# The state-space pipeline of a hybrid decoder step: output one tick later and into the state's tile, two places for the input product, paired matrices

## Chip, cores, metric

The kernel runs on one core of a Trainium2 chip. The metric is device time in microseconds (us), the median of several runs. One further execution was recorded by the hardware profiler; all rows shown come from it.

## What is computed

One inference step of a decoder layer over 2048 + 16 prompt positions and 8 running sequences of 8 tokens, 1024 channels, in fp32. An input projection gives six streams. One of them goes through a state-space branch (64 groups of 16 channels, 64 complex states each), one through a pooling branch (causal means over 2, 4, 8 or 16 positions, one window for each quarter of the channels); gates, two branch projections and an output projection follow.

```
...
    bu_re = jnp.einsum('blgc,gpc->lbgp', uf, bbar_re)
...
    _, _, s_re, s_im = lax.associative_scan(
        _complex_scan_combine, (a_seq_re, a_seq_im, bu_re, bu_im), axis=0)
...
    y = (jnp.einsum('lbgp,gcp->blgc', s_re, c_re.astype(f32))
         - jnp.einsum('lbgp,gcp->blgc', s_im, c_im.astype(f32)))
    y = y.reshape(bsz, seq_len, D_SSM) + d.astype(f32) * uf.reshape(bsz, seq_len, D_SSM)
...
        win = (cs[:, POOL_BUF + 1:POOL_BUF + 1 + seq_len, lo:hi]
               - cs[:, POOL_BUF + 1 - w:POOL_BUF + 1 - w + seq_len, lo:hi])
...
    merged = g_s * (a @ w_branch_ssm) + g_p * (b @ w_branch_pool)
    return h + merged @ w_out, new_re, new_im, new_buf
```

## The kernel before

**Units.** Positions are folded into chunks of T = 8 and cut into four column groups (`g0` to `g3`, some 512 to 544 columns each). The program is a list of some 340 units written out by hand; nearly all are one 128-row block of one projection for one column group: 8 blocks of the inner dimension, three matmuls each in a split of the weights into a high and a low part (`wh`, `wl`; L128, L130, L132), each matmul in two column halves. TensorE goes through the units in order. What follows a unit (activations, gates, splits) is written on ScalarE, VectorE and GpSimd at the start of the next one; some more work is hung at fractions of a unit. Each engine works strictly in the order in which its instructions were written, and SyncE issues all DMAs in one queue.

**Ticks.** The state-space branch runs beside the units as a software pipeline over 32 pairs of groups, in two rounds (the first for the columns of `g0`, `g1`, the second for `g2`, `g3` and the running sequences). A tick is one step of that pipeline and works on several pairs at once, each at another stage; 37 ticks a round are spread over the units by `spread`. In a unit with one tick, its EARLY part is written after a quarter of the unit's matmuls and its LATE part after the last. What a pair q goes through (number: ticks after its first):

- 0: `st_phase` (GpSimd), LATE `st_wrap` (VectorE), `st_load` (DMAs of the input `su` and the matrix `smb`)
- 1: `st_sin` (ScalarE), LATE `st_x`: the input product, four matmul records into PSUM tile `sx`
- 2: `st_turn_a` copies `sx` with its halves swapped (ScalarE L519, L520; in the second round also L522, the running sequences' part `xs`), `st_turn_v` multiplies `sx` by the cosines (VectorE L528), `st_turn_g` the copy by the sines (GpSimd); LATE `st_scan` (VectorE)
- 3: `st_swap` (ScalarE L546, L547, and the DMA of the matrices `smc`), LATE `st_rot` (VectorE)
- 4: `st_state` (GpSimd) writes the states `sS`, LATE `st_y`: `sy` = matrix times input (L577) plus matrix times state (L578), eight matmul records
- 5: `st_out` copies `sy` to `sY` (ScalarE L582), and a DMA takes that to `ys` in DRAM

In a tick ScalarE has, in this order: L582 for one pair, L546, L547 for a younger one, L519, L520 (L522) for a still younger one, then the sines. VectorE has L528 there. TensorE meets the tick at its LATE part: `st_y` first, then `st_x`. `sx` and `sy` are one PSUM tile each, `sY` and `sS` one SBUF buffer each, `su` four, `smb`, `smc`, `sX` and `sXw` two. Units with two ticks have both in halves of the unit.

**Matrices.** Each group's three 128x128 matrices are made early on, written to `mat_d` in DRAM in 512-byte rows, and read back pair by pair.

**Pooling.** `up_post` builds the window sums by doubling steps on VectorE (L820, L821, L822, L824).

Of the kernel before, what the change touches and what calls it, by code (L numbers as in the profile page):

```python
# [88 lines left out]
def hybrid_step(ctx, tc, a):  # L89
# [74 lines left out]
    mat_d = dram.tile([GRP, P, 3, P], F32, name="mat_d")  # L164
# [181 lines left out]
    def batches(bg):  # L346
# [51 lines left out]
        def s4(b):  # L398
# [9 lines left out]
                          ct[:, i, :, 0:7].rearrange("p c t -> p t c"), start=True, stop=True)  # L408
            d["ps"], d["pk"] = ps, pk

        def s5(b):
# [4 lines left out]
            SY.dma_start(mat_d[gs, :, 0].rearrange("g p m -> p g m"), btT)  # L416
            SY.dma_start(mat_d[gs, :, 2].rearrange("g p m -> p g m"), d["ct"].rearrange("p g c t -> p g (c t)"))
            o = 4 * (b % 2)
            A.activation(d["ks"][:, o:o + 4], d["pk"][:GCH], AF.Copy)

# [16 lines left out]
        def s10(b):  # L437
            o = 4 * (b % 2)
            mt = st.pop(b)["mt"]
            mp = bg.tile([P, 4, P], F32, tag="mp", name="mp")  # L440
            A.activation(mp.rearrange("p g (c t) -> p g c t", t=T),
                         mt[:, o:o + 4].rearrange("p g (t c) -> p g c t", c=GCH), AF.Copy)
            SY.dma_start(mat_d[4 * b:4 * b + 4, :, 1].rearrange("g p m -> p g m"), mp)

        S7 = [(7 + i, lambda b, i=i: s7(b, i)) for i in range(1, NPART)]
        load(0)
# [21 lines left out]
    def stile(tag, bufs, w=NA * NBB):  # L468
        return sw["p"].tile([P, 2, w], F32, tag=tag, bufs=bufs, name=tag)

    def two(q):
        return slice(2 * q, 2 * q + 2)
# [3 lines left out]
        return rows.rearrange("(q c) t k -> (c t) q k", q=2)  # L476

    def st_load(g, q):
        x = stile("su", 4, g.kn + NS)
# [27 lines left out]
    def st_x(g, q):  # L507

        d = pr[q]
        d["px"] = sw["sx"][:, :, :g.kn]  # L510
        for j in range(2):
            PE.matmul(d["px"][:, j], d["mb"][:, j], d["u"][:, j], start=True, stop=True)  # L512

    def st_turn_a(g, q):

        d = pr[q]
        ps, kp = d["px"], g.kp
        xw = stile("sXw", 2, kp)
        A.activation(xw[0:64], ps[64:128, :, :kp], AF.Copy)  # L519
        A.activation(xw[64:128], ps[0:64, :, :kp], AF.Copy)  # L520
        if g.last:
            A.activation(sw["xs"][:, two(q)], ps[:, :, kp:], AF.Copy)  # L522
        d["xw"] = xw

    def st_turn_v(g, q):
# [17 lines left out]
    def st_swap(g, q):  # L543
        d = pr[q]
        z, zw = d["x"], stile("sXw", 2, g.kp)
        A.activation(zw[0:64], z[64:128], AF.Copy)  # L546
        A.activation(zw[64:128], z[0:64], AF.Copy)  # L547
        d["xw"] = zw
        d["m"] = stile("smc", 2, 2 * P)
        SY.dma_start(d["m"].rearrange("p q (j m) -> p q j m", j=2),  # L550
                     mat_d[two(q), :, 1:3].rearrange("q p j m -> p q j m"))

    def st_rot(g, q):

# [5 lines left out]
    def st_state(g, q):  # L560

        d = pr[q]
        c, w, kp = d["c"], d["s"], g.kp
        s = stile("sS", 1, g.kn)
        now = state[:, two(q)].unsqueeze(2)
        if g.last:
            G.tensor_copy(s[:, :, kp:], d["s0"])
        G.tensor_copy(s[:, :, 0:1], now)
        G.tensor_tensor(s[:, :, 1:kp], c[:, :, 1:kp], w[:, :, 1:kp], ALU.subtract)  # L569
        G.tensor_tensor(now, c[:, :, kp:kp + 1], w[:, :, kp:kp + 1], ALU.subtract)  # L570
        d["S"] = s

    def st_y(g, q):
        d = pr[q]
        d["py"] = sw["sy"][:, :, :g.kn]
        for j in range(2):
            PE.matmul(d["py"][:, j], d["m"][:, j, :P], d["u"][:, j], start=True, stop=False)  # L577
            PE.matmul(d["py"][:, j], d["m"][:, j, P:], d["S"][:, j], start=False, stop=True)  # L578

    def st_out(g, q):  # L580
        y = stile("sY", 1, g.kn)
        A.activation(y, pr.pop(q)["py"], AF.Copy)  # L582
        SY.dma_start(chans(g, ys_d, q), y)

    EARLY = ((5, st_out), (3, st_swap), (2, st_turn_a), (1, st_sin), (4, st_state),
             (0, st_phase), (2, st_turn_v), (2, st_turn_g))
    LATE = ((3, st_rot), (0, st_wrap), (2, st_scan), (4, st_y), (1, st_x), (0, st_load))
    NTICK = NPAIR + 5  # L590
# [5 lines left out]

    def final_states():
        SY.dma_start(a["fin"], state)
        for j in range(2):
            s0 = tmp.tile([P, GRP, NS], F32, tag="po", bufs=2, name="s0")  # L600
            SY.dma_start(s0, a["s0"][:, j])
            G.tensor_tensor(s0, s0, a8[:, j].unsqueeze(2).to_broadcast([P, GRP, NS]), ALU.mult)
            G.tensor_tensor(sw["xs"], sw["xs"], s0, ALU.add)
        SY.dma_start(a["fins"], sw["xs"])

    mid = []

# [7 lines left out]
    class Group:  # L615
# [177 lines left out]
        def up_post(self, fb, ps):  # L793
            wi = fb // 2
            kn, kp, last = self.kn, self.kp, self.last
            ke = 2 + kp + (3 * NS if last else 0)
            E = self.t(tmp, "E", 2, shape=[P, T, ke])
            tn = T // self.nh
            if last:
                es = E[:, :, 2 + kp:].rearrange("p t (s k) -> p t s k", k=3)  # L800
                G.tensor_copy(es[:, :, :, 0:2], self.hs.pop(fb))
            for h in range(self.nh):
                src = ps[:, h, :self.N].rearrange("p (t k) -> p t k", k=kn)
                A.activation(E[:, h * tn:(h + 1) * tn, 2:2 + kp], src[:, :, :kp], AF.Copy)
                if last:
                    A.activation(es[:, h * tn:(h + 1) * tn, :, 2:3], src[:, :, kp:].unsqueeze(3), AF.Copy)
            G.tensor_copy(E[:, :, 0:2], hist[:, fb])  # L807
            if last:
                new = self.t(tmp, "np", 2, shape=[P, T, 2 + NS])
                G.tensor_copy(new[:, :, 0:2], E[:, :, kp:kp + 2])  # L810
                G.tensor_copy(new[:, :, 2:].unsqueeze(3), es[:, :, :, 2:3])
                SY.dma_start(a["np"][:, fb], new)
            else:
                G.tensor_copy(hist[:, fb], E[:, :, kp:kp + 2])
            cur = E
            for step in range(wi + 1):
# [597 lines left out]
```

## Time and profile before

| | |
|---|---|
| median of 3 runs | 2157.99 us (2157.77 to 2158.32) |
| profiled execution, its own time | 2159.06 us |
| its span, first to last instruction | 2157.3 us |
| TensorE busy | 2086.0 us, 97% |
| VectorE, GpSimd, ScalarE busy | 1395.2, 923.7, 686.8 us |

The profiled execution lies 1.1 us above the median, and 1.8 us of it lie outside the span. A wait in the profile is idle time of an engine just before an instruction, and is put down to what came last before that instruction could start.

### The profile page before, as it was taken

The numbers are of one execution on the slowest core, as the hardware profiler recorded it, in microseconds if no ns is written. First come the engines' busy times: TensorE is split into PE (matmuls) and PEld (weight loads), VectorE is DVE, ScalarE is ACT, GpSimd is POOL, SyncE is SP. The second block draws the span as 40 slices with busy tenths as digits, with TensorE's granted clock in tenths as the row PEclk, the third lists the DMA queues.
The fourth block names the chain that finished last, engine by engine and source line by source line (L and its number), as shares of the span: only waits on it lengthen the run. The fifth ranks groups of instructions, "written<-read, shape, count | busy, mean of one in ns | idle before, by whom it ended". The sixth has DMA issues, their size and how long they took to land.

```text
span 2157.3 us, 37693 instructions
## 1 busy us (share of the span) xinstructions
PE 2086.0 (97%) x14968; PEld 1970.9 (91%) x14968; DVE 1395.2 (65%) x1916; ACT 686.8 (32%) x1243; POOL 923.7 (43%) x1054
## 2 busy tenths in 40 slices
PE   7999999889899999999899999999999999999998
PEld 7988899888799999999899999999999987888887
DVE  7989968878656686644856676633633767456444
ACT  3213357645434332144544432121210221112101
POOL 3387747565444452233544452233421333244222
PEclk9999999999999999999999999999999999999999
DMA  6646556486944453244444543234333443343223
GB/s 199 145 117 165 164 169 200 144 202 155 183 127 124 151 144 120 89 121 137 120 125 144 157 139 125 82 119 118 104 100 109 144 128 120 101 133 117 91 97 105
DMA packets 261279, 287.77 MB, mean 133 GB/s; under 512 B 106096, under 2 KB 203760, under 8 KB 261104
## 3 DMA queue, kind: packets, MB, share of 16 engines
q1 hardware_dynamic: 261104, 285.37, 45.7%
q8 instruction: 118, 1.93, 0.4%
q14 instruction: 57, 0.47, 0.1%
HBM read 242.32 MB, written 40.62 MB: 131 GB/s over the span
## 4 chain that ended last, share of the span: by engine, by line
PE 71%; DVE 6%; DMA 4%; ACT 3%; issue 2%; POOL 2%; SPq 0%; DVEq 0%; ACTq 0%; POOLq 0%
PE acc L128 23%; PE acc L132 23%; PE acc L130 23%; DMA ys<-sY 1%; DVE wl L206 1%; DVE sX L537 1%; PE sy L578 1%; PE sx L512 1%; PE sy L577 1%; DVE sX L540 1%; DMA raw<-in_wb 1%; DVE al L114 1%; DVE sph L558 1%; DMA mat_d<-mp 1%; DVE sph L499 0%
## 5 line engine op out<-in xcount | busy, mean ns | idle before, releaser
L128 PE MATMUL acc<-ah,wh 128*128 128x268 f32 (+4 forms) x4504 | 1058.9, 305 | 8.9 <-ACT ah L705 6.6
L132 PE MATMUL acc<-ah,wl 128*128 128x268 f32 (+4 forms) x4504 | 1049.0, 302 | 3.7 <-DVE wl L206 3.7
L130 PE MATMUL acc<-al,wh 128*128 128x268 f32 (+4 forms) x4504 | 1047.9, 302 | 0.0
L103 POOL TENSOR_SCALAR wh<-raw 128x1024 fp32r<-128x1024 f32 (+1 forms) x336 | 392.5, 1168 | 969.9 <-PE acc L130 869.7
L128 PEld LDWEIGHTS acc<-ah,wh 128*128 128x128 f32 x4504 | 729.3, 190 | 44.2 <-issue 7.8
L132 PEld LDWEIGHTS acc<-ah,wl 128*128 128x128 f32 x4504 | 727.8, 189 | 32.0 <-DVE wl L206 4.7
L130 PEld LDWEIGHTS acc<-al,wh 128*128 128x128 f32 x4504 | 728.2, 190 | 27.0 <-DVE al L706 0.3
L206 DVE TENSOR_TENSOR wl<-raw,wh 128x1024 fp32r<-128x1024 f32 (+1 forms) x336 | 432.3, 1288 | 140.9 <-POOL wh L103 136.1
L896 ACT ACTIVATE sg<-acc,hb 128x536 f32<-128x536 f32 (+2 forms) x64 | 45.0, 702 | 402.2 <-PE acc L132 402.1
L528 DVE TENSOR_TENSOR sX<-sx,scc 128x270 f32<-128x270 f32 (+1 forms) x64 | 27.2, 424 | 107.3 <-ACT xs L522 65.0
L114 DVE TENSOR_TENSOR al<-H,ah 128x536 fp32r<-128x536 f32 (+3 forms) x96 | 89.3, 963 | 6.8 <-POOL ah L103 5.2
L952 DVE SCALAR_TENSOR_TENSOR H<-po,H 128x536 f32<-128x536 f32 (+2 forms) x32 | 23.8, 745 | 103.4 <-ACT po L950 103.4
L853 ACT ACTIVATE H<-acc 128x536 f32<-128x536 f32 (+2 forms) x64 | 39.1, 610 | 140.9 <-PE acc L132 140.7
L105 ACT ACTIVATE ah<-H 128x536 fp32r<-128x536 f32 (+3 forms) x80 | 50.8, 646 | 92.6 <-DVE H L884 77.1
L854 DVE SCALAR_TENSOR_TENSOR H<-H,acc 128x536 f32<-128x536 f32 (+2 forms) x64 | 44.8, 700 | 48.1 <-ACT H L853 47.6
L577 PE MATMUL sy<-su,smc 128*128 128x135 f32 (+1 forms) x256 | 52.2, 285 | 18.7 <-ACT sY L582 15.7
L820 DVE TENSOR_TENSOR w<-E 128x483 f32<-128x483 f32 (+2 forms) x32 | 21.9, 685 | 73.4 <-POOL E L807 58.0
L963 DVE SCALAR_TENSOR_TENSOR sg<-sg,acc 128x536 f32<-128x536 f32 (+2 forms) x32 | 22.4, 700 | 70.9 <-PE acc L132 70.9
L540 DVE TENSOR_TENSOR_SCAN sX<-r,state,sX 128x135 f32<-128x135 f32 (+1 forms) x128 | 65.7, 554 | 2.3
L950 ACT ACTIVATE po<-acc,hb 128x536 f32<-128x536 f32 (+2 forms) x32 | 22.5, 704 | 134.8 <-PE acc L132 134.8
L905 DVE SCALAR_TENSOR_TENSOR G<-sg,acc 128x536 f32<-128x536 f32 (+2 forms) x32 | 22.4, 699 | 64.9 <-PE acc L132 64.9
L578 PE MATMUL sy<-sS,smc 128*128 128x135 f32 (+1 forms) x256 | 53.1, 290 | 11.2 <-POOL sS L569 11.2
(232 smaller groups left out, 2227.8 us busy)
## 6 DMA issues: line engine op xcount, KB each, us to landing
raw<-in_wb SPq DMA_DIRECT2D x318, 512.0 KB, 3.8
smc<-mat_d SPq DMA_DIRECT2D x64, 256.0 KB, 4.1
smb<-mat_d SPq DMA_DIRECT2D x64, 128.0 KB, 3.3
xr<-in_xb SPq DMA_DIRECT2D x21, 268.0 KB, 4.4
H<-in_xb SPq DMA_DIRECT2D x19, 268.0 KB, 4.4
su<-us SPq DMA_DIRECT2D x32, 135.0 KB, 4.1
ys<-sY SPq DMA_DIRECT2D x32, 135.0 KB, 4.6
us<-po SPq DMA_DIRECT2D x16, 268.0 KB, 6.6
```

Source lines behind the costliest of these rows:

```text
L103: G.tensor_scalar(out, in_, 1.0, 0.0, ALU.mult, ALU.add)
L105: A.activation(out, in_, AF.Copy)
L114: V.tensor_tensor(l, x, h.bitcast(F32), ALU.subtract)
L128: PE.matmul(out, wh, xh, start=first, stop=False)
L130: PE.matmul(out, wh, xl, start=False, stop=False)
L132: PE.matmul(out, wl, xh, start=False, stop=last)
L206: V.tensor_tensor(l[:, c], r[:, c], h[:, c].bitcast(F32), ALU.subtract)
L540: V.tensor_tensor_scan(x[:, j], r8[:, i].to_broadcast([P, g.kp]), x[:, j], state[:, i], ALU.mult, ALU.add)
L577: PE.matmul(d["py"][:, j], d["m"][:, j, :P], d["u"][:, j], start=True, stop=False)
L578: PE.matmul(d["py"][:, j], d["m"][:, j, P:], d["S"][:, j], start=False, stop=True)
L854: V.scalar_tensor_tensor(self.v3(out), self.v3(out), 1.0, self.pv(ps), ALU.add, ALU.mult)
L896: A.activation(self.v3(s), self.pv(ps), AF.Tanh, scale=0.5, bias=hb[:, b, fb:fb + 1])
```

## The change

1. `st_y` moves from stage 4 to 5 and `st_out` from 5 to 6; the load of `smc` leaves `st_swap` and becomes `st_mat` at stage 4, at the end of EARLY. A round has 38 ticks.
2. `st_out` writes into the pair's own `sS` tile in place of a tile `sY`. `sS` has three buffers, `su` five.
3. `st_x` uses two places in turn. One PSUM tile `bk` of two banks (512 fp32 columns each) replaces `sx` and `sy`: columns 0 to 319 of bank 0 and of bank 1 are the two `sx`, columns 320 to 479 of both banks are `sy` (one group of the pair in each).
4. `mat_d` keeps the two groups of a pair side by side (rows of 1024 bytes, `smc` 2048).
5. The running sequences' `xs` goes through small tiles to DRAM (32 more DMAs in round two), and is read back at the end.
6. In `up_post` the first two doubling steps add flat ranges, the others leave out columns that are not used, and the copies at L822 go.

```diff
+    mat_d = dram.tile([GRP // 2, P, 3, 2, P], F32, name="mat_d")
+    xs_d = dram.tile([P, GRP, NS], F32, name="xs_d")
...
     def st_x(g, q):
...
-        d["px"] = sw["sx"][:, :, :g.kn]
+        d["px"] = sw["sx"][q % 2][:, :2 * g.kn].rearrange("p (q k) -> p q k", q=2)
...
         if g.last:
-            A.activation(sw["xs"][:, two(q)], ps[:, :, kp:], AF.Copy)
+            xs = stile("sxs", 2, NS)
+            A.activation(xs, ps[:, :, kp:], AF.Copy)
+            SY.dma_start(xs_d[:, two(q)], xs)
...
+    def st_mat(g, q):
+        d = pr[q]
         d["m"] = stile("smc", 2, 2 * P)
...
-        s = stile("sS", 1, g.kn)
+        s = stile("sS", 3, g.kn)
...
     def st_out(g, q):
-        y = stile("sY", 1, g.kn)
-        A.activation(y, pr.pop(q)["py"], AF.Copy)
+        d = pr.pop(q)
+        y = d["S"]
+        A.activation(y, d["py"], AF.Copy)
         SY.dma_start(chans(g, ys_d, q), y)
...
-    EARLY = ((5, st_out), (3, st_swap), (2, st_turn_a), (1, st_sin), (4, st_state),
-             (0, st_phase), (2, st_turn_v), (2, st_turn_g))
-    LATE = ((3, st_rot), (0, st_wrap), (2, st_scan), (4, st_y), (1, st_x), (0, st_load))
-    NTICK = NPAIR + 5
+    EARLY = ((6, st_out), (3, st_swap), (2, st_turn_a), (1, st_sin), (4, st_state),
+             (0, st_phase), (2, st_turn_v), (2, st_turn_g), (4, st_mat))
+    LATE = ((3, st_rot), (0, st_wrap), (2, st_scan), (5, st_y), (1, st_x), (0, st_load))
+    NTICK = NPAIR + 6
...
+                if d < 4:
+                    n, o, c = (x.rearrange("p t k -> p (t k)") for x in (nxt, cur, cur))
+                    i = d * ke + step
+                    V.tensor_tensor(n[:, i:], o[:, i:], c[:, step:T * ke - d * ke], ALU.add)
...
-        for n in ("sx", "sy"):
-            sw[n] = ps.tile([P, 2, 160], F32, name=n)
-        sw["xs"] = sw["p"].tile([P, GRP, NS], F32, name="xs")
+        bk = ps.tile([P, 2, 512], F32, name="bk")
+        sw["sx"] = [bk[:, j, :320] for j in range(2)]
+        sw["sy"] = bk[:, :, 320:480]
```

What TensorE is told to wait for changes too. First the LATE part of one tick of round one on TensorE, before: `st_y` waits for ScalarE (the copy out of `sy`) and GpSimd (the states), `st_x` for VectorE (L528). A name in brackets is the engine, or the DMA landing, that an instruction waits for.

```order
L577 MATMUL sy<-su,smc 128x135 [waits DMAHW1_49,Activation_49]
L578 MATMUL sy<-sS,smc 128x135 [waits Pool_49]
L577 MATMUL sy<-su,smc 128x135
L578 MATMUL sy<-sS,smc 128x135
L512 MATMUL sx<-su,smb 128x135 [waits DMAHW3_49,DMAHW2_49,DVE_49]
L512 MATMUL sx<-su,smb 128x135
```

The same place of the changed program:

```order
L587 MATMUL bk<-su,smc 128x135 [waits DMAHW7_49,DVE_49]
L588 MATMUL bk<-sS,smc 128x135 [waits Pool_49]
L587 MATMUL bk<-su,smc 128x135
L588 MATMUL bk<-sS,smc 128x135
L517 MATMUL bk<-su,smb 128x135 [waits DMAHW1_49,DMAHW0_49]
L517 MATMUL bk<-su,smb 128x135
```

The wait for VectorE has moved from `st_x` to the first matmul of `st_y`, where it stands in the place of the wait for ScalarE; `st_x` waits for its DMAs alone.

GpSimd at a tick's EARLY part, before (`sS` one buffer) and then of the changed program (three buffers):

```order
L568 COPY sS<-state 128x2 [waits PE_49]
L569 TENSOR_TENSOR sS<-scc,sph 128x2x134 [waits DVE_49]
L570 TENSOR_TENSOR state<-scc,sph 128x2 [waits Pool_49]
L490 TENSOR_TENSOR sph<-pA,pB 128x272 [waits Pool_49]
L493 TENSOR_SCALAR scc<-sph 128x272 [waits Pool_49]
L532 TENSOR_TENSOR sXw<-sXw,sph 128x270 [waits DVE_49,Activation_49]
```

```order
L577 COPY sS<-state 128x2 [waits DMAHW6_49]
L578 TENSOR_TENSOR sS<-scc,sph 128x2x134 [waits DVE_49]
L579 TENSOR_TENSOR state<-scc,sph 128x2 [waits Pool_49]
L495 TENSOR_TENSOR sph<-pA,pB 128x272 [waits Pool_49]
L498 TENSOR_SCALAR scc<-sph 128x272 [waits Pool_49]
L539 TENSOR_TENSOR sXw<-sXw,sph 128x270 [waits DVE_49,Activation_49]
```

Here the wait for TensorE has become one for a landing: that of the `ys` transfer which reads the buffer that `sS` takes over.

With 38 ticks in place of 37 the ticks also stand beside other units. ScalarE in `g0`'s output projection, before (`po<-G` squares a finished block, `ah<-H` splits the next group's normed input, then a tick begins with the copy out of `sy`):

```order
L989 ACTIVATE po<-G_4104 128x528
L105 ACTIVATE ah<-H_8378 128x536
L105 ACTIVATE ah<-H_8494 128x536
L989 ACTIVATE po<-G_4353 128x528
L105 ACTIVATE ah<-H_8609 128x536
L105 ACTIVATE ah<-H_8685 128x536
L582 ACTIVATE sY<-sy 128x262
```

and in the changed program:

```order
L1006 ACTIVATE po<-G_4114 128x528
L105 ACTIVATE ah<-H_8328 128x536
L105 ACTIVATE ah<-H_8489 128x536
L593 ACTIVATE sS<-bk 128x262
```

The tick that stood behind the splits `H_8609`, `H_8685` (the fourth pair of them) now stands behind the third pair, one unit earlier.

## Rows read from the trace of the kernel before

**Rows 1.** The page: busy time, share of the span and instructions of two engines.

```profile
PE 2086.0 (97%) x14968; PEld 1970.9 (91%) x14968; DVE 1395.2 (65%) x1916; ACT 686.8 (32%) x1243; POOL 923.7 (43%) x1054
```

**Rows 2.** TensorE's waits: us in total, times, longest us.

```profile
PE sy L577 <- ACT sY L582: 15.7, 8, 3.3
PE sy L578 <- POOL sS L569: 11.2, 11, 1.7
PE sx L512 <- DVE sX L528: 10.4, 10, 2.2
...
PE sy L577 <- DMA smc<-mat_d: 2.9, 3, 1.3
...
PE sx L512 <- DMA smb<-mat_d: 1.0, 1, 1.0
```

**Rows 3.** Windows: PE, PEld, DVE, ACT, POOL busy us (instructions), granted clock, DMA.

```profile
558.90:565.70 6.80, 6.19 (x17) 5.14 (x18) 4.13 (x9) 2.10 (x6) 2.56 (x6) 0.50 0.77 134
...
sum 33.70, PE 30.64 PEld 28.98 DVE 26.72 ACT 15.95 POOL 19.71; mean PE 5.11 PEld 4.83 DVE 4.45 ACT 2.66 POOL 3.29
```

**Rows 4.** TensorE's timeline, a tick without a wait: start, length, instruction, records.

```profile
1219.39 0.39 PE L577 MATMUL sy<-su,smc 128*128 128x131 f32 x2
...
1220.29 0.61 PE L512 MATMUL sx<-su,smb 128*128 128x131 f32 x4
```

**Rows 5.** TensorE's timeline, a tick of round two in `g0`'s output projection.

```profile
789.66 0.49 PE L577 MATMUL sy<-su,smc 128*128 128x131 f32 x2 [2.02 <-ACT sY L582]
791.77 0.80 PE L578 MATMUL sy<-sS,smc 128*128 128x131 f32 x2 [1.61 <-POOL sS L569]
```

**Rows 6.** ScalarE's timeline in that tick, its first instruction.

```profile
789.24 0.37 ACT L582 ACTIVATE sY<-sy 128x262 f32<-128x262 f32 x1
```

**Rows 7.** VectorE's timeline in that tick.

```profile
791.47 0.41 DVE L528 TENSOR_TENSOR sX<-sx,scc 128x246 f32<-128x246 f32 x1 [0.46 <-ACT xs L522]
```

**Rows 8.** TensorE's timeline, a tick of round one, the first of 19 that wait.

```profile
348.61 0.47 PE L577 MATMUL sy<-su,smc 128*128 128x135 f32 x2 [0.64 <-DMA smc<-mat_d]
...
350.51 0.73 PE L512 MATMUL sx<-su,smb 128*128 128x135 f32 x4 [0.74 <-DVE sX L528]
```

**Rows 9.** ScalarE's timeline in that tick.

```profile
347.88 0.40 ACT L582 ACTIVATE sY<-sy 128x270 f32<-128x270 f32 x1 [3.01 <-DMA ys<-sY]
```

**Rows 10.** VectorE's timeline in that tick: the scans before it, and L528.

```profile
346.15 1.24 DVE L540 TENSOR_TENSOR_SCAN sX<-r,state,sX 128x135 f32<-128x135 f32 x2
350.01 0.44 DVE L528 TENSOR_TENSOR sX<-sx,scc 128x270 f32<-128x270 f32 x1 [2.62 <-ACT sXw L520]
```

**Rows 11.** TensorE's timeline, the last of the 19 ticks.

```profile
1272.59 0.49 PE L577 MATMUL sy<-su,smc 128*128 128x131 f32 x2 [1.58 <-ACT sY L582]
1274.71 0.49 PE L578 MATMUL sy<-sS,smc 128*128 128x131 f32 x2 [1.63 <-POOL sS L569]
```

**Rows 12.** VectorE's timeline in that tick.

```profile
1274.40 0.41 DVE L528 TENSOR_TENSOR sX<-sx,scc 128x246 f32<-128x246 f32 x1 [0.44 <-ACT xs L522]
```

**Rows 13.** ScalarE's waits: us in total, times, longest us.

```profile
ACT sY L582 <- DMA ys<-sY: 35.1, 12, 5.9
```

**Rows 14.** VectorE's waits, the two for ScalarE before L528.

```profile
DVE sX L528 <- ACT xs L522: 65.0, 23, 6.9
...
DVE sX L528 <- ACT sXw L520: 42.3, 25, 5.1
```

**Rows 15.** TensorE's timeline at the end of a unit, where now a tick ends.

```profile
781.42 0.41 PE L132 MATMUL acc<-ah,wl 128*128 128x264 f32 x2
```

**Rows 16.** ScalarE's timeline in that unit, the splits that precede the tick.

```profile
781.63 1.34 ACT L105 ACTIVATE ah<-H 128x536 fp32r<-128x536 f32 x2
```

**Rows 17.** VectorE's copies at L822: duration ns min/median/max, first and last start.

```profile
L822 DVE COPY w<-w x40: 154/161/1025, 156.9 to 1836.0; 128x2 f32<-128x2 f32 x24, 128x4 f32<-128x4 f32 x16
L822 DVE COPY w<-E x32: 135/140/147, 130.7 to 1834.0; 128x1 f32<-128x1 f32 x32
```

More of the change, by code (lines that the diff above doesn't have):

```diff
@@ L163, in hybrid_step @@
     rs_d = [dram.tile([P, T * kn], F32, name=f"rs{i}") for i, (_, kn) in enumerate(GROUPS)]
-    mat_d = dram.tile([GRP, P, 3, P], F32, name="mat_d")
+    mat_d = dram.tile([GRP // 2, P, 3, 2, P], F32, name="mat_d")
+    xs_d = dram.tile([P, GRP, NS], F32, name="xs_d")
     psum = ctx.enter_context(tc.tile_pool(name="psum", bufs=1, space=PSUM))
@@ L409, in s4, with mat_store @@
             d["ps"], d["pk"] = ps, pk
+        def mat_store(b, j, x):
+            SY.dma_start(mat_d[2 * b:2 * b + 2, :, j].rearrange("q p g m -> p q (g m)"),
+                         x.rearrange("p (q g) m -> p q (g m)", g=2))
         def s5(b):
@@ L415, in s5 @@
             A.activation(btT, d["ps"], AF.Copy)
-            SY.dma_start(mat_d[gs, :, 0].rearrange("g p m -> p g m"), btT)
-            SY.dma_start(mat_d[gs, :, 2].rearrange("g p m -> p g m"), d["ct"].rearrange("p g c t -> p g (c t)"))
+            mat_store(b, 0, btT)
+            mat_store(b, 2, d["ct"].rearrange("p g c t -> p g (c t)"))
             o = 4 * (b % 2)
@@ L442, in s10 @@
                          mt[:, o:o + 4].rearrange("p g (t c) -> p g c t", c=GCH), AF.Copy)
-            SY.dma_start(mat_d[4 * b:4 * b + 4, :, 1].rearrange("g p m -> p g m"), mp)
+            mat_store(b, 1, mp)
         S7 = [(7 + i, lambda b, i=i: s7(b, i)) for i in range(1, NPART)]
@@ L478, in st_load @@
     def st_load(g, q):
-        x = stile("su", 4, g.kn + NS)
+        x = stile("su", 5, g.kn + NS)
         u = x[:, :, :g.kn]
@@ L484, in st_load @@
         mb = stile("smb", 2, P)
-        SY.dma_start(mb, mat_d[two(q), :, 0].rearrange("q p m -> p q m"))
+        SY.dma_start(mb, mat_d[q, :, 0])
         pr[q].update(u=u, mb=mb, s0=x[:, :, g.kn:])
@@ L548, in st_swap @@
         d["xw"] = zw
+    def st_mat(g, q):
+        d = pr[q]
         d["m"] = stile("smc", 2, 2 * P)
-        SY.dma_start(d["m"].rearrange("p q (j m) -> p q j m", j=2),
-                     mat_d[two(q), :, 1:3].rearrange("q p j m -> p q j m"))
+        SY.dma_start(d["m"], mat_d[q, :, 1:3].rearrange("p j q m -> p j (q m)"))
     def st_rot(g, q):
@@ L576, in st_y @@
         for j in range(2):
-            PE.matmul(d["py"][:, j], d["m"][:, j, :P], d["u"][:, j], start=True, stop=False)
-            PE.matmul(d["py"][:, j], d["m"][:, j, P:], d["S"][:, j], start=False, stop=True)
+            m = slice(j * P, (j + 1) * P)
+            PE.matmul(d["py"][:, j], d["m"][:, 0, m], d["u"][:, j], start=True, stop=False)
+            PE.matmul(d["py"][:, j], d["m"][:, 1, m], d["S"][:, j], start=False, stop=True)
     def st_out(g, q):
-        y = stile("sY", 1, g.kn)
-        A.activation(y, pr.pop(q)["py"], AF.Copy)
+        d = pr.pop(q)
+        y = d["S"]
+        A.activation(y, d["py"], AF.Copy)
         SY.dma_start(chans(g, ys_d, q), y)
-    EARLY = ((5, st_out), (3, st_swap), (2, st_turn_a), (1, st_sin), (4, st_state),
-             (0, st_phase), (2, st_turn_v), (2, st_turn_g))
-    LATE = ((3, st_rot), (0, st_wrap), (2, st_scan), (4, st_y), (1, st_x), (0, st_load))
-    NTICK = NPAIR + 5
+    EARLY = ((6, st_out), (3, st_swap), (2, st_turn_a), (1, st_sin), (4, st_state),
+             (0, st_phase), (2, st_turn_v), (2, st_turn_g), (4, st_mat))
+    LATE = ((3, st_rot), (0, st_wrap), (2, st_scan), (5, st_y), (1, st_x), (0, st_load))
+    NTICK = NPAIR + 6
     def tick(steps, g, i):
@@ L598, in final_states @@
         SY.dma_start(a["fin"], state)
+        xs, s0 = (tmp.tile([P, GRP, NS], F32, tag="po", bufs=2, name="s0") for _ in range(2))
+        SY.dma_start(xs, xs_d)
         for j in range(2):
-            s0 = tmp.tile([P, GRP, NS], F32, tag="po", bufs=2, name="s0")
             SY.dma_start(s0, a["s0"][:, j])
             G.tensor_tensor(s0, s0, a8[:, j].unsqueeze(2).to_broadcast([P, GRP, NS]), ALU.mult)
-            G.tensor_tensor(sw["xs"], sw["xs"], s0, ALU.add)
-        SY.dma_start(a["fins"], sw["xs"])
+            G.tensor_tensor(xs, xs, s0, ALU.add)
+        SY.dma_start(a["fins"], xs)
     mid = []
@@ L818, in up_post @@
                 nxt = self.t(tmp, f"w{step % 2}", 1, shape=[P, T, ke])
+                if d < 4:
+                    n, o, c = (x.rearrange("p t k -> p (t k)") for x in (nxt, cur, cur))
+                    i = d * ke + step
+                    V.tensor_tensor(n[:, i:], o[:, i:], c[:, step:T * ke - d * ke], ALU.add)
+                elif d < T:
+                    V.tensor_tensor(nxt[:, d:, 1:], cur[:, d:, 1:], cur[:, :T - d, 1:], ALU.add)
+                else:
+                    V.tensor_tensor(nxt[:, :, 2:], cur[:, :, 2:], cur[:, :, 1:ke - 1], ALU.add)
                 if d < T:
-                    V.tensor_tensor(nxt[:, d:], cur[:, d:], cur[:, :T - d], ALU.add)
                     V.tensor_tensor(nxt[:, :d, 1:], cur[:, :d, 1:], cur[:, T - d:, :ke - 1], ALU.add)
-                    V.tensor_copy(nxt[:, :d, 0:1], cur[:, :d, 0:1])
-                else:
-                    V.tensor_tensor(nxt[:, :, 1:], cur[:, :, 1:], cur[:, :, :ke - 1], ALU.add)
                 cur = nxt
```

## The prediction

> **What bounds the kernel now.** I read the page first: TensorE is busy 97% of the span, the next engine 65% [rows 1]. The end is TensorE's, so I look only at what keeps TensorE idle or slow. Its list of waits comes next. Five entries belong to the pipeline that is changed: 15.7 + 11.2 + 10.4 + 2.9 + 1.0 = 41.2 us [rows 2]. Third, the granted clock. The six stretches at which it was 0.50 inside the two rounds, so 1.2 in place of 2.4 GHz, hold 30.64 us of busy TensorE [rows 3]; at the full level that work takes half, so they cost 15.3 us, 2.6 each. Each lies in or right behind a tick in which TensorE had waited 2.8 to 4.2 us. At stake are 41.2 + 15.3 = 56 us, 2.6%.
>
> Then single ticks in the timelines. In a tick without a wait `st_y` takes 1220.29 - 1219.39 = 0.90 us, and `st_x` follows at once [rows 4]. Of the ticks, 19 wait in or after `st_y` and hold 39.7 of the 41.2 us (the rest is in the first two `st_x`). In the one at 789 TensorE arrived at 789.66 - 2.02 = 787.64 and waited 2.02 and 1.61 us [rows 5]. ScalarE's copy began only at 789.24, behind work of the output projection [rows 6], and L528 ended at 791.47 + 0.41 = 791.88 [rows 7]. So L528 ends 2.64 us after that copy begins, since four or five ScalarE instructions stand between. That distance is what the reader should keep.
>
> **The change, part by part.**
>
> *The state a tick earlier.* `st_state` now has a whole tick more before `st_y` needs it, and the 11.2 us for GpSimd go. At 789 it was 1.61 us late, against ticks that are 6 us and more apart.
>
> *The two places for the input product.* The changed program's rows are plain: `st_x` no longer waits for VectorE, and `st_y` does. L535, the turn that was L528, is the only VectorE instruction that touches `bk`, and the one waited for is that of the same tick. Before, `st_y` could run while the turn was still to come, and 0.90 us of it hid under that wait. Now `st_y` itself starts after the turn. `sy` lies in both banks, so whichever half of `bk` the turn reads, `st_y` writes beside it.
>
> What this costs is worked out tick by tick: the new wait is the later of the end of L528 and the landing of `smc`, less TensorE's arrival. At 789: 791.88 - 787.64 = 4.24 us, against 2.02 + 1.61 = 3.63 now [rows 5, 7]. In the first of the 19: arrival 348.61 - 0.64 = 347.97, turn over at 350.45, so 2.48 against 0.64 + 0.74 = 1.38 [rows 8, 10]. In the last: 1274.81 - 1271.01 = 3.80 against 3.21 [rows 11, 12]. All 19 done like this give 58.3 us in place of 39.7.
>
> The Trainium skill's page "Perfetto Trace Analysis", section "Matmuls", asks that independent matmul groups rotate through PSUM banks so that the evacuation of one lies beside the next. By that rule the change should win the 10.4 us and more. Its page "PSUM — Partial Sum Buffer", section "PSUM bank collisions raise a hardware error", says that two engines must not be in one bank at once, and that speaks against sharing each bank between `sx` and `sy`. The trace of before has `sx` and `sy` apart and shows neither; the changed order agrees with the second page.
>
> *The output without its own buffer.* ScalarE's copy out of `sy` waited 35.1 us, 12 times, for the last `ys` transfer to land [rows 13], and with it the turn copies behind it and L528, which waits for ScalarE [rows 14]. That wait now sits on GpSimd, ahead of the state, the next phases and the sine turn. So ScalarE is early in those ticks, but not by the whole wait: the swap comes first and needs the scan of the tick before. In the first of the 19 the copy waited 3.01 us [rows 9], while the scans ended at 346.15 + 1.24 = 347.39 [rows 10]; two swaps, two turn copies and L528 (2.2 us) put the turn's end at 349.6, a wait of 1.6 us, not 2.48. Taken so in all 12 ticks, 58.3 falls to 49.3; with nothing early it stays 58.3, with the whole 35.1 us early it is 45.6. I take 49.3. About 1 us each comes on top for six ticks that wait little or not at all today, and for the first `smb`. Together 51.3 against 41.2: **+10 us** (+6 to +19).
>
> *Other places of the ticks.* With 38 ticks a round, round two's ticks stand beside other units. In the output projection one moves to a unit whose splits end at 781.63 + 1.34 = 782.97 [rows 16]; 2.64 us later the turn is over, at 785.6, while TensorE arrives 0.25 us after 781.42 [rows 15]: 3.9 us, about what the old place costs. In the next group's output projection a tick falls on the same kind of unit where none waited (+3.1); in that group's SSM gates the places shift by one unit each, and one of the three ticks has no wait today; for it I add 2 us, between nothing and the 3.9 above. Against that, about 1 us less in the tick behind the new wait. **+4 us** (0 to +6).
>
> *The clock.* Nine ticks would now wait 3 us or more in one piece, where six stretches at 1.2 GHz lie today. Three more at 2.6 us: **+7 us** (0 to +15).
>
> *Side by side in DRAM, `xs` through DRAM, pooling.* The landing of `smc` and `smb` accounts for 2.9 + 1.0 us of waits [rows 2]; half as many and longer rows can win at most that, and the landings hide behind the turn in most ticks. The 32 new transfers of `xs` stand ahead of `smc`, but `smc` has a tick more than it needs in round two. The copies at L822 are 40 of 161 and 32 of 140 ns [rows 17], some 11 us of VectorE at stages where TensorE waits a few microseconds in all. Taken together **-2 us** (-5 to +1); if a flat sum were slower than its 3D form, VectorE's third of idle time [rows 1] takes it.
>
> *Catching up.* A longer wait in one tick lets the other engines run ahead before the next: **-3 us** (-8 to 0).
>
> The sum is 10 + 4 + 7 - 2 - 3 = +16 us. On the profiled execution's 2159.06 that is 2175; on the median 2157.99, which lies 1.1 us lower, **2174 us**, +0.7%.
>
> **The rivals.**
>
> *ScalarE's early start reaches everything (faster).* If in round one the scans come earlier too, because ScalarE no longer holds the pipeline, L528 ends before TensorE arrives, and only `smc` landings are left there. Round one's waits then fall from 26 to about 8 us and two of its three slow stretches go (-5); round two stays +5, +4 and +3 with the clock. Sum -11, 2147 us. It decides from the point where the turn ends over 2 us earlier than now in the ticks around 350 to 560. For it: 35.1 us are a lot. Against: GpSimd's sine turn, on which the scan waits, now stands behind the landing instead, and those 12 landings leave ticks in which ScalarE was late without any DMA, as at 789 [rows 6].
>
> *The two places work as meant (faster).* If `st_y` waited for ScalarE alone, 11.2 + 10.4 us would go and about three slow stretches with them (-8): 2128 us. The program's own order speaks against it.
>
> *Names change, the sum does not.* The turn bounds TensorE today (through `st_x`) and afterwards (through `st_y`); with 45.6 us, no extra slow stretch and catching up in full it is +4, -2 and -3: 2157 us.
>
> *All upper bounds (slower).* No early ScalarE (+19), six more from the places, +12 by the clock: 2193 us.
>
> **How the numbers follow.** About 0.2%, 4.3 us, is what a measurement of this kernel can tell from no change. The forecast, 2163 to 2186, has a chance of 0.50; the slow rival, above 2186, 0.18; the same within 4.3 us, 0.17; the two fast ones 0.12 and 0.03. So slower 0.68, same 0.17, faster 0.15. The range leaves out the fast rivals' far parts and the top: 2150 to 2192; the forecast's own range is 2163 to 2186.
>
> **What would show it.** In TensorE's waits after, the entry for ScalarE's `sY` and that for GpSimd's `sS` are gone or under 1 us, and `bk` at L587 waiting for VectorE's `sX` at L535 heads the list with 35 to 55 us; `st_x` at L517 waits only for DMAs. ScalarE's wait for `ys` landings is gone, and GpSimd's first instruction of the state has one of 20 us or more. Around 780 to 800 and 1260 to 1290 the waits are 3 to 4 us in one piece. The 0.50 stretches inside the rounds hold over 33.7 us. The forecast is wrong if L587's waits add up to less than 30 us, or if stretches at 0.50 become fewer: then the turn comes earlier than I let it.

## The result, and the profile after

| | before | after |
|---|---|---|
| median of 5 runs each | 2158.32 us | 2169.06 us (2167.34 to 2173.35) |
| ratio, 95% interval | | 1.0051 (1.0036 to 1.0066) |
| profiled execution, its span | 2159.06, 2157.3 us | 2167.34, 2165.6 us |

The changed kernel is 0.5% slower, some 11 us. The forecast was 2174 us, 2150 to 2192, slower with 0.68.

The page's busy times after, against [rows 1]:

```profile
PE 2087.4 (96%) x14968; PEld 1974.4 (91%) x14968; DVE 1389.2 (64%) x1844; ACT 686.3 (32%) x1243; POOL 929.7 (43%) x1054
```

TensorE is busy 1.4 us more, VectorE has lost 72 small copies; of the 8.3 us by which this span is the longer one, 6.9 are idle time of TensorE. Its waits (us in total, times, longest), against [rows 2]:

```profile
PE bk L587 <- DVE sX L535: 30.3, 16, 3.7
PE acc L128 <- ACT ah L717: 6.5, 2, 6.2
PE bk L587 <- DMA smc<-mat_d: 6.2, 3, 2.5
PE acc L128 <- DVE po L782: 5.7, 1, 5.7
PE bk L517 <- DVE sX L535: 4.2, 2, 3.6
...
PE bk L587 <- ACT sS L593: 2.9, 1, 2.9
...
PE acc L128 <- ACT ah L105: 1.6, 1, 1.6
...
PE bk L517 <- DMA smb<-mat_d: 0.6, 1, 0.6
```

The five entries of the pipeline add up to 30.3 + 6.2 + 4.2 + 2.9 + 0.6 = 44.2 us, against 41.2: 3.0 more. The wait for the turn (L535) now stands at L587, the first matmul of `st_y`, as the order of the program said. The largest other change is an entry outside the pipeline: 5.7 us, once, for VectorE's copy of a finished block (`po`, L782; 0.4 us before).

The ten stretches at a granted clock of 0.50 inside the two rounds (380 to 384, 445 to 449, 469 to 472, 486 to 490, 496 to 503, 558 to 561, 667 to 670, 787 to 793, 1036 to 1039, 1281 to 1288), their sum by windows, against [rows 3]:

```profile
sum 43.80, PE 37.26 PEld 37.10 DVE 38.05 ACT 14.37 POOL 22.96; mean PE 3.73 PEld 3.71 DVE 3.81 ACT 1.44 POOL 2.30
```

37.26 us of TensorE at 1.2 GHz cost half of that, 18.6 us, against 15.3 before: +3.3.

The tick in `g0`'s output projection that [rows 5 to 7] showed at 789, in the timelines of TensorE, VectorE and ScalarE after (start, length, instruction, wait):

```profile
787.25 0.81 PE L587 MATMUL bk<-su,smc 128*128 128x131 f32 x2 [3.71 <-DVE sX L535]
...
786.78 0.41 DVE L535 TENSOR_TENSOR sX<-bk,scc 128x246 f32<-128x246 f32 x1 [0.46 <-ACT sxs L528]
...
784.55 0.37 ACT L593 ACTIVATE sS<-bk 128x262 f32<-128x262 f32 x1
```

From ScalarE's copy out to the end of the turn it is 786.78 + 0.41 - 784.55 = 2.64 us, as before; TensorE waits 3.71 us in one piece where it waited 2.02 and 1.61.

The wait for the landing of `ys`, which was ScalarE's [rows 13], in GpSimd's waits:

```profile
POOL sS L577 <- DMA ys<-sS: 35.9, 11, 6.9
```

And what precedes the 5.7 us, on VectorE and then on TensorE:

```profile
494.88 0.89 DVE L504 SCALAR_TENSOR_TENSOR sph<-scc,sph 128x272 f32<-128x272 f32 x1 [2.19 <-POOL scc L498]
495.69 1.27 DVE L544 TENSOR_TENSOR sX<-sX,sXw 128x270 f32<-128x270 f32 x1
497.00 0.89 DVE L547 TENSOR_TENSOR_SCAN sX<-r,state,sX 128x135 f32<-128x135 f32 x2
497.80 1.20 DVE L207 TENSOR_TENSOR wl<-raw,wh 128x1024 fp32r<-128x1024 f32 x1
498.92 0.71 DVE L782 TENSOR_TENSOR po<-acc,rs 128x536 f32<-128x536 f32 x1
...
499.77 0.78 PE L128 MATMUL acc<-ah,wh 128*128 128x264 f32 x2 [5.66 <-DVE po L782]
```

VectorE's wrap waits for GpSimd's phases, which stand behind the state; behind the wrap stand the scan, a weight split and only then the copy that gives TensorE its accumulator back.

### The profile page after: what moved, and what is told of

Read it like the earlier page. It is cut to its first block, busy times and chain, and to the rows that moved or that the text cites. A ratio compares the mean times of both kernels' runs of the same rounds, so it can differ in the third digit from the quotient of the medians.

```text
span 2165.6 us, 37736 instructions
## 1 busy us (share of the span) xinstructions
PE 2087.4 (96%) x14968; PEld 1974.4 (91%) x14968; DVE 1389.2 (64%) x1844; ACT 686.3 (32%) x1243; POOL 929.7 (43%) x1054
## 3 DMA queue, kind: packets, MB, share of 16 engines
q1 hardware_dynamic: 237184, 285.89, 45.3%
## 4 chain that ended last, share of the span: by engine, by line
PE 67%; DVE 3%; ACT 1%; POOL 1%; issue 1%; DMA 0%; DVEq 0%; SPq 0%; POOLq 0%; ACTq 0%
PE acc L128 22%; PE acc L132 22%; PE acc L130 22%; PE bk L587 1%; DVE al L114 1%; PE bk L588 1%; PE bk L517 1%; DVE wl L207 0%; DVE w L950 0%; DMA smc<-mat_d 0%; DVE sX L544 0%; POOL wh L103 0%; DVE xr L954 0%; POOL ss L1010 0%; DVE H L771 0%
## 5 line engine op out<-in xcount | busy, mean ns | idle before, releaser
L128 PE MATMUL acc<-ah,wh 128*128 128x268 f32 (+4 forms) x4504 | 1060.1, 305 | 15.3 <-ACT ah L717 6.5
L587 PE MATMUL bk<-su,smc 128*128 128x135 f32 (+1 forms) x256 | 55.7, 300 | 39.5 <-DVE sX L535 30.3
L535 DVE TENSOR_TENSOR sX<-bk,scc 128x270 f32<-128x270 f32 (+1 forms) x64 | 27.1, 423 | 91.3 <-ACT sxs L528 61.8
L587 PEld LDWEIGHTS bk<-su,smc 128*128 128x128 f32 x256 | 41.8, 201 | 45.8 <-DVE sX L535 34.8
L504 DVE SCALAR_TENSOR_TENSOR sph<-scc,sph 128x272 f32<-128x272 f32 x64 | 48.1, 752 | 27.3 <-POOL scc L498 27.3
```

Of the source, the lines that this page charges most:

```text
L128: PE.matmul(out, wh, xh, start=first, stop=False)
L504: V.scalar_tensor_tensor(ph, pr[q]["c"], -MAGIC, ph, ALU.add, ALU.subtract)
L587: PE.matmul(d["py"][:, j], d["m"][:, 0, m], d["u"][:, j], start=True, stop=False)
```

## The experiments

All are compared with the kernel before, run beside them; on these chips its median was 2160 to 2163 us, so the ratios are what is read. Their intervals are 0.1 to 0.15% either way; a difference of two ratios is known to about 0.17%, 4 us. The changed kernel and its variants ran on several chips, each beside the kernel before on the same chip; that the ratios carry over from one chip to another is assumed.

Three theories to begin with. **S**: the two shared banks make `st_y` wait for the turn, and that is the loss. **L**: the loss is the landing that now holds GpSimd. **P**: the loss is the places that 38 ticks take. A fourth, **M**, which comes up later, puts the loss on items 4 to 6 of the change.

**own_tiles.** The changed kernel with tiles of their own for `sx` and `sy`.

```diff
-        bk = ps.tile([P, 2, 512], F32, name="bk")
-        sw["sx"] = [bk[:, j, :320] for j in range(2)]
-        sw["sy"] = bk[:, :, 320:480]
+        for n in ("sx", "sy"):
+            sw[n] = ps.tile([P, 2, 160], F32, name=n)
```

> The changed kernel with sx and sy as two PSUM tiles of their own, as before the change; everything else of the change stays. Theory S (the shared banks make st_y itself wait for the turn): st_y runs under the wait for the turn again, up to 0.90 us a tick. Over the waits at L587 in the changed kernel's trace the smaller of the wait and 0.90 us adds up to 16 us, some 12 of it in ticks that wait for the turn. With two slow stretches fewer (-5 us): 2152 us (2146 to 2158), TensorE waits of the pipeline near 30 in place of 44 us. Theory L (the landing of ys, now waited for on GpSimd, makes the turn late): the wait only moves back to st_x, 2164 to 2170 us. Theory P (the places of 38 ticks cost the time): as L.

Measured: 1.0026 (1.0016 to 1.0037), 2168.09 us. Half the loss goes, half stays. TensorE's waits in the pipeline still add up to 38 us, with 0.7 for `smb`:

```profile
PE sy L587 <- ACT sS L593: 13.6, 8, 3.2
PE sx L517 <- DVE sX L535: 13.2, 14, 3.6
PE sy L587 <- DMA smc<-mat_d: 10.8, 5, 3.4
```

The wait has split into its old two places, and the matrices' landing appears.

**halves.** One tile for each bank, and TensorE's order turned, so that a half of `st_y` and `st_x` run ahead of the wait for the turn.

```diff
-    LATE = ((3, st_rot), (0, st_wrap), (2, st_scan), (5, st_y), (1, st_x), (0, st_load))
+    LATE = ((3, st_rot), (0, st_wrap), (2, st_scan), (5, st_y0), (1, st_x), (5, st_y1), (0, st_load))
```

> The changed kernel with each of the two banks as a tile of its own, and TensorE's order in a tick turned: first the half of st_y in the bank that is not being turned, then st_x in that same bank, then the other half of st_y. ScalarE's copy out is two instructions (+0.2 us a tick ahead of the turn copies). Theory S: 0.45 + 0.61 = 1.06 us of work stands ahead of the wait for the turn in each tick; 16 to 18 us of waits go, some 3 come back by ScalarE's longer copy, and two slow stretches less: 2151 us (2144 to 2158). Theory L or P: what is waited for is as late as before, the waits in a tick keep their sum less a few us: 2163 to 2169 us.

Measured: 1.0023 (1.0014 to 1.0032). The wait for the turn falls from 30.3 to 8.4 us, but ScalarE and the landing of `smc` end last instead:

```profile
PE bk L586 <- ACT sS L599: 15.7, 8, 2.8
PE bk L586 <- DMA smc<-mat_d: 10.3, 4, 4.2
PE bk L586 <- DVE sX L535: 8.4, 10, 1.3
```

As with tiles of their own, a quarter of a per cent is to be had, no more.

**before_bk.** The kernel before with the shared banks alone.

```diff
+        bk = ps.tile([P, 2, 512], F32, name="bk")
+        sw["sx"] = [bk[:, j, :320] for j in range(2)]
+        sw["sy"] = bk[:, :, 320:480]
...
-        d["px"] = sw["sx"][:, :, :g.kn]
+        d["px"] = sw["sx"][q % 2][:, :2 * g.kn].rearrange("p (q k) -> p q k", q=2)
```

> The kernel before with the one tile of two banks alone (two places for sx, sy across both). Theory S: st_y waits for the turn of its own tick, and ScalarE still waits for the landings ahead of it; worked out tick by tick from the rows of before the waits grow from 39.7 to 58.3 us, the other engines take back some 3, two to three slow stretches come on top: 2178 us (2170 to 2184). Theory L or P: the turn bounds the tick wherever TensorE meets it, 2156 to 2163 us.

Measured: 1.0002 (0.9993 to 1.0011). Alone, the shared banks cost nothing, so theory S does not explain the whole loss; the half that own_tiles gained has to come from the banks together with the rest of the change. The wait itself came. In the tick that was at 789 and in the last of the 19 it is as worked out (4.24 and 3.80 us), in the first it is shorter (2.48):

```profile
351.85 0.50 PE L577 MATMUL bk<-su,smc 128*128 128x135 f32 x2 [1.93 <-DVE sX L528]
...
796.97 0.63 PE L577 MATMUL bk<-su,smc 128*128 128x131 f32 x2 [4.29 <-DVE sX L528]
...
1277.86 0.49 PE L577 MATMUL bk<-su,smc 128*128 128x131 f32 x2 [3.85 <-DVE sX L528]
```

But the sum did not:

```profile
PE bk L577 <- DVE sX L528: 42.5, 19, 4.6
PE bk L578 <- POOL sS L569: 1.2, 1, 1.2
PE bk L512 <- DMA smb<-mat_d: 0.9, 1, 0.9
PE bk L512 <- DVE sX L528: 0.7, 1, 0.7
```

These are 45.3 us, where the ticks worked out one by one gave 58.3 and the first two `st_x` some 1.4. By round, some 38 us worked out for the 14 ticks of round one became 26.1, and 20.4 for the five of round two became 17.6. Three of those five held to 0.1 us. In three pairs of ticks 7 to 17 us apart the second waited much less than worked out (0.47, 1.21 and 2.36 us in place of 2.78, 3.89 and 4.72), as if the longer wait in one tick were in part paid back in the next.

**landing_aside.** The changed kernel, GpSimd's sine turn ahead of the state and the wrap behind the scan.

```diff
-    EARLY = ((6, st_out), (3, st_swap), (2, st_turn_a), (1, st_sin), (4, st_state),
-             (0, st_phase), (2, st_turn_v), (2, st_turn_g), (4, st_mat))
-    LATE = ((3, st_rot), (0, st_wrap), (2, st_scan), (5, st_y), (1, st_x), (0, st_load))
+    EARLY = ((6, st_out), (3, st_swap), (2, st_turn_a), (1, st_sin),
+             (2, st_turn_v), (2, st_turn_g), (4, st_state), (0, st_phase), (4, st_mat))
+    LATE = ((3, st_rot), (2, st_scan), (0, st_wrap), (5, st_y), (1, st_x), (0, st_load))
```

> The changed kernel with GpSimd's sine turn written ahead of the state (which waits for the ys landing) and with the wrap written behind the scan on VectorE, so that turn and scan no longer stand behind the landing. Theory S: the wait for the turn stays; the 5.7 us at 499 (VectorE's copy of a finished block behind that chain) and a few waits of ticks may go: 2160 to 2167 us. Theory L: the early ScalarE now reaches the turn everywhere, L587's waits in round one fall from 24 to under 10 us: below 2157 us. Theory P: 2167 to 2170 us.

Measured: 1.005 (1.0036 to 1.0064), no change. GpSimd's wait for the landing falls from 35.9 to 9.8 us, but now it waits for ScalarE's copies ahead of the sine turn, with state and phases behind it (14.6 us in the changed kernel):

```profile
POOL sXw L539 <- ACT sXw L525: 99.5, 54, 7.1
POOL sS L577 <- DMA ys<-sS: 9.8, 3, 5.8
```

One wait has taken the place of another, so this does not decide on L.

**before_38.** The kernel before with one empty tick more.

```diff
-    NTICK = NPAIR + 5
+    NTICK = NPAIR + 6
```

> The kernel before with 38 ticks a round in place of 37, the last one empty: only the places of the ticks beside the units change. Theory S (the shared banks) fell with the run that had them alone. Theory P (the places cost the time): the waits of round two grow by some 5 us, as in the changed kernel, and TensorE waits some 5 us near 495 for the copy of a finished block (L770): ratio 1.003 to 1.005 to the kernel before. Theory L (the landing of ys on GpSimd, and smc a tick later): within 0.1% of before. Theory M (the matrices side by side, xs through DRAM, the pooling sums): within 0.1% of before.

Measured: 1.0033 (1.002 to 1.0046). Theory P: the places alone cost 7 us. In the profiled execution these are not the ticks' own waits (40.5 us in all), but the copy of a finished block and, in the sum over the twelve 0.50 stretches inside its rounds, the clock (46.23 us of TensorE at 1.2 GHz against 30.64):

```profile
PE acc L128 <- DVE po L770: 4.5, 1, 4.5
...
PE acc L128 <- ACT ah L105: 1.5, 1, 1.5
...
sum 50.00, PE 46.23 PEld 44.10 DVE 42.24 ACT 22.11 POOL 29.18; mean PE 3.85 PEld 3.67 DVE 3.52 ACT 1.84 POOL 2.43
```

**rest.** The kernel before with items 4 to 6 of the change alone (matrices, `xs`, pooling); the lines are those of the change's diff, of which two stand here.

```diff
-    mat_d = dram.tile([GRP, P, 3, P], F32, name="mat_d")
+    mat_d = dram.tile([GRP // 2, P, 3, 2, P], F32, name="mat_d")
+    xs_d = dram.tile([P, GRP, NS], F32, name="xs_d")
```

> The kernel before with items 4 to 6 alone: matrices of a pair side by side in DRAM, xs through DRAM, the pooling sums without copies (and the load of smc at the end of its EARLY part, in the same tick). 37 ticks, sY and sx, sy as before. Theory M: ratio 1.002 to 1.005. Theories P and L, and the forecast's own term of -2 us: 0.998 to 1.0005.

Measured: 0.9998 (0.9989 to 1.0006). These items are worth nothing that can be measured.

**after_37 and own_37.** The changed kernel with 37 ticks: `st_y` at stage 4 and the output at stage 5, as before. The second one has tiles of their own for `sx` and `sy` too (the diff of own_tiles).

```diff
-    EARLY = ((6, st_out), (3, st_swap), (2, st_turn_a), (1, st_sin), (4, st_state),
-             (0, st_phase), (2, st_turn_v), (2, st_turn_g), (4, st_mat))
-    LATE = ((3, st_rot), (0, st_wrap), (2, st_scan), (5, st_y), (1, st_x), (0, st_load))
-    NTICK = NPAIR + 6
+    EARLY = ((5, st_out), (3, st_swap), (2, st_turn_a), (1, st_sin), (4, st_state),
+             (0, st_phase), (2, st_turn_v), (2, st_turn_g), (3, st_mat))
+    LATE = ((3, st_rot), (0, st_wrap), (2, st_scan), (4, st_y), (1, st_x), (0, st_load))
+    NTICK = NPAIR + 5
```

> The changed kernel with 37 ticks: st_y at stage 4 and the output at stage 5 again, smc loaded at the end of EARLY of stage 3. The output still goes into sS, the two banks are shared, items 4 to 6 stay. Theory P: the ticks stand at the places of before, 0.999 to 1.001 times before; the wait near 499 is gone. Theory L: the sS buffer now has two ticks from its output to its next state in place of one, so the landing hurts less, 1.001 to 1.003. Theory M: 1.003 to 1.005.

> As the changed kernel with 37 ticks, and with sx and sy as two PSUM tiles of their own. ScalarE's copy out no longer waits for the landing of the tick before (35.1 us on ScalarE before), st_y may lie under the wait for the turn. Theory P: 0.995 to 0.999 times before, since ScalarE's early start in round one is then all that is left of the change. Theory L: 1.001 to 1.003. Theory M: 1.002 to 1.005.

Measured: 0.9971 (0.996 to 0.9982) and **0.9948** (0.9934 to 0.9961; 2152.75 us beside 2162.55). Both are faster than the kernel before, the first by more than any of the theories had it, and the second is the best version found. In neither do ScalarE and GpSimd wait for the landing of `ys`: an `sS` buffer of three is filled with the next states two ticks after its output, not one.

Against `rest`, `own_37` differs in the output into `sS` with three buffers and in `su` of five: together 0.50%. The second difference is not idle. With four `su` the DMA queue (SPq, where all transfers stand in line) has to wait at the load of `su` until `st_y` gives a buffer back, 112 us in `rest`; with five and the tick later it waits again; in `own_37` and `after_37` that entry is gone. First the kernel before, then `places_37` (below):

```profile
SPq L481 <- PE sy L577: 130.0, 28, 10.1
SPq L481 <- PE sy L578: 31.7, 22, 4.4
```

```profile
SPq L486 <- PE bk L588: 133.8, 43, 9.1
```

So two waits came and went together, the landing of `ys` and the queue's for `su`, and no run has only one of them. TensorE's entries for landings of matrices did not fall with the queue's wait (2.9 us in `rest`, 6.7 in `own_37`); those for ScalarE, GpSimd and the turn did (37.9 to 27.8). That speaks for the landing of `ys` but does not show it. What TensorE still waits for in `own_37`, and its nine stretches at 1.2 GHz:

```profile
PE sy L587 <- ACT sS L593: 11.0, 6, 3.3
PE sy L588 <- POOL sS L578: 10.7, 11, 1.7
...
PE sx L517 <- DVE sX L535: 6.1, 4, 2.2
PE sy L587 <- DMA smc<-mat_d: 3.9, 3, 2.5
PE sx L517 <- DMA smb<-mat_d: 2.8, 2, 1.9
```

```profile
sum 36.50, PE 34.38 PEld 33.20 DVE 29.97 ACT 15.01 POOL 24.24; mean PE 3.82 PEld 3.69 DVE 3.33 ACT 1.67 POOL 2.69
```

The waits are 34.5 us, 6.7 fewer than before; the clock gives nothing (34.38 us against 30.64). These two runs change stage and places together, and the next ones part them. **Q** is the rival that the tick later itself costs.

**places_37, round1_37 and own_places_37.** The changed kernel with the 37 places of before and the last tick in the unit behind them: in both rounds, in round one only, and in both with tiles of their own.

```diff
-            while n < NTICK and (n + 0.5) * total < done * NTICK:
+            while n < NTICK - 1 and (n + 0.5) * total < done * (NTICK - 1):
                 ticks.setdefault(i, []).append((r, n))
                 n += 1
+        ticks.setdefault(hi, []).append((r, n))
```

In round one only:

```diff
+            nt = NTICK - (r.i == 0)
-            while n < NTICK and (n + 0.5) * total < done * NTICK:
+            while n < nt and (n + 0.5) * total < done * nt:
                 ticks.setdefault(i, []).append((r, n))
                 n += 1
+        if n < NTICK:
+            ticks.setdefault(hi, []).append((r, n))
```

> The changed kernel, whole, with its first 37 ticks of each round at the places of the kernel before and the 38th (which only copies out the last pair) in the unit behind them. Theory P (the places of the ticks cost the time): as the run with 37 ticks, 0.996 to 0.999 times before; no wait of 5 us near 499, none for L105's splits near 1245. Rival Q (the tick that st_y and the output come later costs it: smc held longer, sS held until the landing): 1.003 to 1.006, as the changed kernel.

> As the run before it, but only round one has the places of before; round two keeps those of the change. Theory P: of what the places cost, the waits and slow stretches of the traces put half on each round: 1.000 to 1.003. If round one holds nearly all: 0.996 to 0.999; if round two does: 1.004 to 1.006. Rival Q: 1.003 to 1.006.

> The changed kernel with the 37 places and one behind, and with sx and sy as two PSUM tiles of their own. Theory P: at least as good as the run with 37 ticks and tiles of their own (0.9948), less GpSimd's 10.7 us of waits at the state that this had, of which the turn takes back most: 0.992 to 0.996. Rival Q: 0.999 to 1.003.

Measured: 1.0008 (1.0 to 1.0017), 1.0032 (1.002 to 1.0044) and 0.997 (0.9958 to 0.9982). P and Q are both right in part: the places cost 1.0051 - 1.0008 = 0.43%, about half of it in each round (0.19 and 0.24%, hardly more than these runs can tell), and the tick later 1.0008 - 0.9971 = 0.37% (0.22% with tiles of their own, just above what these runs can tell). In `places_37` GpSimd waits for the landing again, and the copy of a finished block is no longer late:

```profile
POOL sS L577 <- DMA ys<-sS: 33.5, 9, 7.1
```

```profile
PE acc L128 <- DVE po L782: 0.4, 1, 0.4
```

**one_moved.** The changed kernel with tick 27 of round one back in its old unit.

```diff
+        if r.i == 0:
+            i = hi - NB
+            ticks[i].insert(0, ticks[i - 3].pop())
```

> The changed kernel with one tick moved: tick 27 of round one from the last unit of g2's `us` to the first unit of g3's, where it stood before. Theory P in its narrow form (this one place makes VectorE's copy of a finished block late, 5.7 us near 499, and a slow stretch of 3.3 us behind it): 1.001 to 1.003. In its wide form (many places, each a little): 1.004 to 1.0055. Rival Q: 1.004 to 1.006.

Measured: 1.0054 (1.004 to 1.0069). The 5.7 us wait falls to 2.2, and the time does not follow:

```profile
PE acc L128 <- DVE po L782: 2.2, 1, 2.2
```

The narrow form of P falls. Its profiled execution, 2165.4 us, is the fastest of six (the others 2171.9 to 2177.3), so its rows can't say where the other runs lost the time again.

## Why the prediction was right, and where its sum was not

One chain of runs takes the change apart, each step a difference of ratios (times 2158 us):

| step | runs | measured |
|---|---|---|
| items 4 to 6 | before, rest | -0.02%, 0 us |
| output into `sS`, three buffers, `su` of five | rest, own_37 | -0.50%, -11 us |
| shared banks | own_37, after_37 | +0.23%, +5 us |
| everything a tick later | after_37, places_37 | +0.37%, +8 us |
| the places of 38 ticks | places_37, after | +0.43%, +9 us |

The direction was right, and the time lay 5 us from the forecast, but the split was not: errors of both signs cancelled, and that it came so near is luck. By the terms for waits, places and catching up the pipeline's waits should have grown by 10 + 4 - 3 = 11 us; in the profile they grew by 3.0, and most of the loss stands elsewhere.

*`st_y` waits for the turn: right, and priced too high.* The row is there and heads the list, with 30.3 us in 16 ticks where 35 to 55 were named as the sign, at 787 with 3.71 us where 3.9 was worked out. The step that failed is "worked out tick by tick": 58.3 us for a kernel with the old landings became 45.3 in `before_bk`. The term of **catching up**, -3, was mis-sized; there it is about 58.3 + 1.4 - 45.3 = 14 us. The 51.3 holds only 2 us for the six further ticks and the first `smb`; at about 1 us each, as its sentence reads, they would be 7. What the shared banks cost hangs on the rest: nothing on the kernel before, 0.23 to 0.38% in the kernels whose output goes into `sS` (own_37, own_tiles and own_places_37 against their partners). The Trainium skill's page "PSUM — Partial Sum Buffer", section "PSUM bank collisions raise a hardware error", fits what the program orders here only in part: `st_y` does wait for the reader of the other columns, but not by bank. Its first matmul always writes the first bank, the turn reads the two banks in alternate ticks, and in two successive ticks that first matmul waits all the same:

```profile
459.39 0.50 PE L587 MATMUL bk<-su,smc 128*128 128x135 f32 x2 [0.57 <-DVE sX L535]
...
469.62 0.59 PE L587 MATMUL bk<-su,smc 128*128 128x135 f32 x1 [2.64 <-DVE sX L535]
```

In one of the two the turn reads the other bank, so the wait goes with the tile `bk`; halves, with a tile for each bank, is free of that for the first half of `st_y`. The rotation that its page "Perfetto Trace Analysis", section "Matmuls", asks for gains where TensorE's order uses the bank that is free (halves, 0.28% under the changed kernel), and no more than two tiles of their own do without it (0.25%).

*The output without its own buffer: right in place, its size open.* GpSimd has the wait, 35.9 us where 20 or more were expected. The forecast gave the early ScalarE 58.3 - 49.3 = 9 us and let it be used up by the wait for the turn. With 37 ticks neither engine waits for the landing and 11 us are won, `su` of five included, which the forecast did not price; the tick later puts 33.5 us of the wait back, and the queue's wait for `su` too. That the tick later costs 8 us is measured; that one of these waits is the cause is only argued, since `st_y` and `smc` move as well.

*The state a tick earlier: right.* The entry for GpSimd's `sS` is gone. What that is worth alone no run shows: in `own_places_37` it is gone too (10.7 us in `own_37`), but the rest of the tick later is in that run as well, and it is no faster.

*Other places of the ticks: mis-sized.* +4 us (0 to +6) was the term, 9 us is the measure, 7 and 12 in two other pairs (before_38; own_tiles against own_places_37). Looking at the ticks' own waits was not enough. The places also make other work late: 5.7 us for `po` and 1.6 us for ScalarE's splits near 1245, both in rows after. One such place moved back did not help, so what each place costs stays open.

*The clock: mis-sized.* +3.3 us in the profiled execution against +7. The term counted ticks that wait 3 us or more in one piece; there were six (3.0 to 3.7 us), not nine, and ten stretches at 1.2 GHz. The count was no measure of them: five lie at or behind such a tick, four at or behind one that waited 2.5 to 2.9 us, one at the 5.7 us for `po`, and the tick at 1075 with 3.3 us has none behind it. The ten cost 1.9 us each, not 2.6.

*Items 4 to 6:* -2 us forecast, 0 measured, within its range. *`st_x` waits for DMAs alone:* right but for the first ticks of a round, which have no `st_y` yet; there `st_x` meets the turn (4.2 us).

Of the rivals, the first fast one was worked out at 2147 us, and 0.9948 times 2158, for `own_37`, is 2147 too. That is a coincidence of numbers. The rival is about the changed kernel and lets round one's waits fall from 26 to about 8 us and two of its three slow stretches go; in `own_37` they fall to 20.8, with four stretches. What the two have in common is that ScalarE is early and no other engine takes its wait over.

## What to carry to other kernels

A buffer that a DMA reads should lie idle until the landing: here three buffers with two ticks between output and refill took 35 us of waits away, the same three with one tick moved them to another engine. Look at the DMA queue's own waits too, and change one buffer count at a time: here `su` of five changed them together with `sS`. One stage more in a pipeline that is spread over other work shifts every tick; look at what those ticks delay outside the pipeline (accumulators that wait to be emptied) and at the clock, not at the pipeline's waits alone. Waits worked out one by one held here in some ticks that stood far from others, and came out too long where ticks are dense; only a run of that part alone told by how much.

## What was not expected of the hardware

Executions of one program lay further apart than was expected, and not by the same amount everywhere: the kernel before lay between 2157.77 and 2159.31 us in five runs on the first chip and between 2159.49 and 2169.12 in 24 on another, `one_moved` between 2165.4 and 2177.3 in six. A few us more or less of waits in one profiled execution are no evidence by themselves here; the ratios are.
